# Second FFN's gate and up: chunks begun with one to three weight tiles, seven block products for one weight tile of seven pairs, x kept in DRAM meanwhile

## Chip, cores and metric

One core of a Trainium2 chip. The metric is the device time of one execution in microseconds (us); less is better. TensorE (PE) multiplies, its weight loads (PEld) overlap its matmuls; VectorE (DVE), ScalarE (ACT) and GpSimd (POOL) do the rest; SyncE (SP) issues the DMAs, in the order of its queue.

## The reference

One block of a transformer on 256 tokens of width D = 2048, all in float32. `c` gives nine vectors (shift, scale, gate for each of three parts) by one product with `w_ada`, 144 rows of 128 values.

```python
ada = silu(c) @ w_ada + b_ada
sh1, sc1, g1, shm, scm, gm, sh2, sc2, g2 = split(ada, 9)
h = rms_norm(x, ffn1_norm) * (1 + sc1) + sh1
x = x + 0.5 * g1 * swiglu(h, ffn1_w_gu, ffn1_w_down)
h = rms_norm(x, mix_norm) * (1 + scm) + shm
x = x + gm * hybrid_mixer(h, ...)        # attention and a causal convolution
h = rms_norm(x, ffn2_norm) * (1 + sc2) + sh2
x = x + 0.5 * g2 * swiglu(h, ffn2_w_gu, ffn2_w_down)

def swiglu(h, w_gu, w_down):             # w_gu 2048 x 11264, w_down 5632 x 2048
    g, u = split(h @ w_gu, 2)
    return (silu(g) * u) @ w_down
```

## The kernel before, in words

Stages: first FFN, mixer, second FFN (`ffn(norm2, ...)`, its modulation rows 96 to 127, its gate's 128 to 143). The change is in the last.

Precision: every operand is split in a high and a low part (`whi`, `wlo` of a weight, `hh`, `hl` of an activation), and a product of a 128x128 block of the activation with a 128x512 block of the weight is three matmuls, high x high, high x low and low x high (`mm3`, L329, L333, L334). ScalarE casts the high half (L305), VectorE subtracts for the low (L307), each for 128x1024, half of a weight tile.

Gate and up: the 11264 columns are 22 chunks of 512 (256 of the gate, 256 of up). A chunk's 2048 rows are four weight tiles `w_gu[c, pc]`, each 1 MB: 128 partitions x 4 x 512, `k` = 4 rows' blocks. A weight tile makes 4 x 2 x 3 = 24 matmuls (`mm_tile`: 4 blocks, 2 halves `t` of the tokens). The first weight tile of a chunk needs only a quarter of the normed activation (`hh[0]`, `hl[0]`), and each further one a quarter more, which needs 8 further rows of the modulation (`ada`, L193: a 1 MB DMA, a multiply and a sum on VectorE; `pieces` and `complete` build the quarter).

In the second FFN all 22 chunks first take their first weight tile (L773), with the sums put away as `parts[c]` (L666); chunks 3, 4 and 5 then take their second (`early`, L798), added by `add_part` (L786). Then `groups` finishes chunk by chunk (L860): remaining weight tiles, then `finish`: sum with the part (L830), silu (L831), product (L832), and, since `CROSSBAR` is on for this FFN, a transposition by DMA: `planes` splits the 16-bit halves (L836), the DMA transposes (L842), ScalarE joins them (L845), `split_from_psum` splits them (L350, L351) into `aT[c]`. `after_tiles(n, fn)` puts `fn` off until n weight tiles have been multiplied. `ada_a` and `ada_b` are the rows of the modulation issued per weight tile in the two parts (0.78, 0.5).

Down product (`down_strassen`): in two passes of 1024 columns over 22 chunks; 7 of them (`SEVEN`) use Winograd's form of Strassen's product, seven block products for eight (21 matmuls for 24), with sums of the activation (`sums_of`), of which `KEPT` are kept for the second pass, and differences of the weights on VectorE (L547 to L550). It adds into x and stores the output.

Buffers: `blk` (28 of 4 KB a partition: parts, normed activation, `aT` and others), `raw` (4, the weight tiles and modulation rows as loaded), `whi` and `wlo` (4 halves each), `tmp` (6), `acc` and `tp` (6 and 2 PSUM banks). x has its own 16 KB (`xall`). The order on each engine is made by a list scheduler from the program order; engines then run their own lists in that order and wait for each other by semaphores.

## Time and profile before

| | |
|---|---|
| median of 3 runs | 1829.34 us (1828.84 to 1831.11) |
| the profiled execution | 1831.11 us, span 1829.3 us |
| granted TensorE clock | 0.999 |
| PE, PEld busy | 1802.8 us (99%), 1484.0 us (81%) |
| DVE, ACT, POOL busy | 1519.9 us (83%), 1008.3 us (55%), 28.3 us (2%) |
| DMA | 501.68 MB, mean 274 GB/s |

The span runs from the first instruction to the last; times in rows are us from its start, means of one instruction in ns. A row of a list of stretches has, for each engine, busy us and in brackets the instructions, then the granted clock, the busy share of the 16 DMA engines and GB/s. A row of a group has the line, the engine, the operation, what it writes and reads, the shape, the count, busy us, mean ns, and idle us before it with what ended it. A row of waits has the waiting engine, tile and line, what it waited for, us in total, times, longest. A row of the timeline has start, duration, engine, line, operation and idle us before it; consecutive instructions of an engine may overlap.

### The profile page before, as it was taken

The page shows a single profiled execution, that of the slowest core. Times are in us where ns is not written, and L with a number is a line of the kernel's source. Part 1 is how long each engine was busy: PE and PEld are TensorE (multiplying, and loading weights), DVE is VectorE, ACT ScalarE, POOL GpSimd, SP SyncE. Part 2 cuts the span into 40 slices and gives each one's busy share as a digit, 9 for nine tenths or more (in the row PEclk, how much of TensorE's full clock was granted, in tenths as well). Part 3 has the DMA queues.
Part 4 walks back from the last instruction along what each step waited for, and adds up shares of the span by engine and source line. Part 5 has one row for each costly group of instructions (what it writes and reads, how often), then busy time and mean ns, then how long its engine had stood idle before and what let it go on. Part 6 is the DMA issues. An engine that isn't in the chain of part 4 may idle for free.

```text
span 1829.3 us, 21896 instructions
## 1 busy us (share of the span) xinstructions
PE 1802.8 (99%) x8117; PEld 1484.0 (81%) x8117; DVE 1519.9 (83%) x2018; ACT 1008.3 (55%) x1521; POOL 28.3 (2%) x29
## 2 busy tenths in 40 slices
PE   7999999999999999999999999999999999999998
PEld 5788888888888887788888787888888888878887
DVE  6889869999898787898999778878887765699877
ACT  6553444444444344566798655664665565555453
POOL 0000000000000000000110100000000000000000
PEclk9999999999999999999999999999999999999999
DMA  9987978888889998775444466889899877655552
GB/s 373 349 307 297 347 274 310 327 314 337 337 330 350 355 343 327 290 261 206 176 147 162 160 254 241 328 337 346 262 313 298 302 242 222 203 207 210 204 214 109
DMA packets 95962, 501.68 MB, mean 274 GB/s; under 512 B 31424, under 2 KB 31856, under 8 KB 38384
## 3 DMA queue, kind: packets, MB, share of 16 engines
q1 hardware_dynamic: 95856, 500.30, 74.4%
q8 instruction: 63, 1.03, 0.2%
q14 instruction: 43, 0.35, 0.1%
HBM read 492.37 MB, written 2.12 MB: 270 GB/s over the span
## 4 chain that ended last, share of the span: by engine, by line
PE 85%; DVE 6%; DMA 4%; ACT 3%; issue 2%; POOL 0%; POOLq 0%; DVEq 0%; SPq 0%; ACTq 0%
PE acc L333 27%; PE acc L334 27%; PE acc L329 27%; DVE wlo L307 2%; DMA tmp<-tmp 1%; DMA xall<-in_x_dram 1%; PE tp L333 1%; PE tp L334 1%; DMA raw<-in_w_ada_dram 1%; PE tp L329 1%; ACT whi L305 1%; PE acc L1137 1%; DVE raw L193 1%; DVE wlo L513 1%; DVE blk L1029 1%
## 5 line engine op out<-in xcount | busy, mean ns | idle before, releaser
L333 PE MATMUL acc<-wlo,blk 128*128 128x512 f32 x2340 | 913.7, 390 | 6.9 <-DVE wlo L307 6.9
L329 PE MATMUL acc<-whi,blk 128*128 128x512 f32 x2343 | 911.4, 392 | 1.9 <-ACT blk L403 1.4
L334 PE MATMUL acc<-whi,blk 128*128 128x512 f32 x2340 | 912.3, 390 | 0.1
L305 ACT CAST whi<-raw 128x1024 fp32r<-128x1024 f32 (+1 forms) x581 | 597.3, 1044 | 473.3 <-PE acc L334 333.9
L307 DVE TENSOR_TENSOR wlo<-raw,whi 128x1024 fp32r<-128x1024 f32 (+1 forms) x581 | 691.1, 1210 | 177.7 <-ACT whi L305 176.6
L333 PEld LDWEIGHTS acc<-wlo,blk 128*128 128x128 f32 x2340 | 439.6, 188 | 103.1 <-DVE wlo L307 12.9
L329 PEld LDWEIGHTS acc<-whi,blk 128*128 128x128 f32 x2343 | 439.9, 188 | 93.4 <-ACT blk L403 1.8
L334 PEld LDWEIGHTS acc<-whi,blk 128*128 128x128 f32 x2340 | 439.3, 188 | 91.9 <-DVE blk L405 0.7
L193 DVE CUSTOM_DVE_ANT_0 raw<-raw,c_bc 128x2048 f32<-128x2048 f32 x142 | 324.2, 2285 | 10.3 <-DMA raw<-in_w_ada_dram 10.3
L512 ACT CAST whi<-raw 128x1024 fp32r<-128x1024 f32 (+1 forms) x56 | 53.0, 947 | 68.4 <-PE tp L334 31.9
L513 DVE TENSOR_TENSOR wlo<-raw,whi 128x1024 fp32r<-128x1024 f32 (+1 forms) x56 | 60.8, 1087 | 19.1 <-ACT whi L512 18.9
L666 ACT COPY blk<-acc 128x512 f32<-128x512 f32 x72 | 42.0, 590 | 62.9 <-PE acc L334 60.2
L1029 DVE SCALAR_TENSOR_TENSOR blk<-blk,cst,blk 128x245 f32<-128x245 f32 (+21 forms) x176 | 70.4, 457 | 0.6 <-ACT blk L1027 0.5
L845 ACT COPY tmp<-tmp 128x1024 uint16<-128x1024 uint16 x22 | 29.8, 1355 | 51.2 <-DMA tmp<-tmp 51.2
L830 DVE TENSOR_TENSOR blk<-acc,blk 128x512 f32<-128x512 f32 x88 | 56.6, 682 | 0.0
L831 ACT ACTIVATE blk<-blk 128x256 f32<-128x256 f32 x88 | 33.7, 413 | 20.5 <-DVE blk L830 20.4
L329 PE MATMUL acc<-blk,blk 128*128 128x512 f32 x104 | 41.3, 401 | 1.2 <-ACT blk L321 1.2
L333 PE MATMUL acc<-blk,blk 128*128 128x512 f32 x100 | 39.1, 391 | 0.6 <-DVE blk L307 0.6
L334 PE MATMUL acc<-blk,blk 128*128 128x512 f32 x100 | 39.0, 392 | 0.0
L351 DVE TENSOR_TENSOR blk<-tmp,blk 128x512 fp32r<-128x512 f32 x22 | 15.1, 688 | 26.0 <-ACT blk L350 26.0
L832 DVE TENSOR_TENSOR blk<-blk 128x256 f32<-128x256 f32 x88 | 33.8, 417 | 0.4 <-ACT blk L831 0.4
L836 ACT COPY tmp<-blk 128x1024 uint16<-128x1024 uint16 x22 | 22.9, 1042 | 14.2 <-DVE blk L832 14.1
(227 smaller groups left out, 1058.7 us busy)
## 6 DMA issues: line engine op xcount, KB each, us to landing
raw<-in_w_gu_dram SPq DMA_DIRECT2D x161, 1024.0 KB, 6.0
raw<-in_w_ada_dram SPq DMA_DIRECT2D x142, 1024.0 KB, 6.3
raw<-in_w_dn_dram SPq DMA_DIRECT2D x88, 1024.0 KB, 5.4
raw<-in_w_in_dram SPq DMA_DIRECT2D x40, 1024.0 KB, 4.8
raw<-in_w_out_dram SPq DMA_DIRECT2D x16, 1024.0 KB, 4.8
raw<-in_w_gu_dram SPq DMA_DIRECT2D x8, 768.0 KB, 6.5
blk<-in_w_gu_dram SPq DMA_DIRECT2D x10, 512.0 KB, 13.5
blk<-gate_line SPq DMA_DIRECT2D x6, 512.0 KB, 4.8
```

Source lines behind the costliest of these rows:

```text
L193: nc.vector.tensor_tensor_reduce(out=raw, in0=raw, in1=c_bc, scale=1.0, scalar=0.0, op0=ALU.mult, op1=ALU.add, accum_out=ada_cols[g][:, j ...
L305: nc.scalar.copy(out=hi[:, :m, :], in_=rw)
L307: nc.vector.tensor_sub(out=lo[:, :m, :], in0=rw, in1=hi[:, :m, :].bitcast(F32))
L329: nc.tensor.matmul(acc, ah, wh, start=start, stop=False)
L333: nc.tensor.matmul(acc, ah, wl, start=False, stop=False)
L334: return nc.tensor.matmul(acc, al, wh, start=False, stop=stop)
L512: nc.scalar.copy(out=hi[:, :n, :], in_=src)
L513: nc.vector.tensor_sub(out=lo[:, :n, :], in0=src, in1=hi[:, :n, :].bitcast(F32))
L666: last_part[0] = nc.scalar.copy(out=parts[c][:, t, :], in_=accs[t])
L830: nc.vector.tensor_add(out=p[:, t, :], in0=accs[t], in1=p[:, t, :])
L832: nc.vector.tensor_mul(out=p[:, t, 256:], in0=p[:, t, :256], in1=p[:, t, 256:])
L1029: nc.vector.scalar_tensor_tensor(out=y[:, d:], in0=u, scalar=w, in1=y[:, d:], op0=ALU.mult, op1=ALU.add)
```

## The change

The second FFN's gate and up take another order. 18 chunks begin with one, two or three weight tiles (`AHEAD_2`) whose sum is put away once; chunks 18 to 21 have no part. The rest goes in the order of `REST_2`. For seven pairs of neighbouring chunks (`PAIRS_2`) the last weight tile (pc = 3) of both is taken first, by `pair_first`: Winograd's seven block products over halves of the tokens, of the rows and of the two chunks; sums of the activation come once from `pair_sums`. Four differences of the weights, seven splits and four partial sums (`kept`, read from a bank that is then added to further) go with it. Odd pairs use two `tp` banks.

`finish` writes the transposition's operands into the chunk's own part, and joins two weight tiles after the DMA (`joined`). x lies in four `blk` buffers (the pool has 32 for 28 and `xall` is gone), loaded in halves; they are written to DRAM during chunks 6 to 9 (`spill`) and fetched back at chunk 16 of each pass of the down product (`fetch`). The modulation's rows come at 0.75 and 0.35 a weight tile, three more during the output projection; from row 32 their bias is added for 8 rows at once, and scales are made for four blocks at once. `KEPT` is 7 for 6. Every other use of `x[n][:, t, :]` becomes `xs(n, t)`; `mm3` and `mm_tile` pass on a flag (`more`) that has no instruction of its own.

```diff
 SEVEN = (3, 5, 8, 10, 13, 15, 17)
-KEPT = 6
+KEPT = 7
 CROSSBAR = {0: False, 96: True}
+AHEAD_2 = (1,) * 10 + (2,) * 4 + (3,) * 4
+REST_2 = (10, 14, 0, 11, 18, 15, 2, 12, 4, 16, 20, 6, 13, 8, 17)
+PAIRS_2 = (0, 2, 4, 6, 8, 18, 20)
...
-    blkp = ctx.enter_context(tc.tile_pool(name="blkp", bufs=28))
+    blkp = ctx.enter_context(tc.tile_pool(name="blkp", bufs=32))
...
-    xall = const.tile([P, NT, D], F32, name="xall")
-    x = [xall[:, :, n * 512:(n + 1) * 512] for n in range(4)]
+    xb = [[blk([P, 1024]) for _ in range(2)] for _ in range(NT)]
+
+    def xs(n, t):
+        return xb[t][n // 2][:, n % 2 * 512:n % 2 * 512 + 512]
+
     first_cols = _COLS["nm"][0]
     nc.sync.dma_start(out=cst[:, :first_cols], in_=small[:, :first_cols])
 
     def load_x(t):
-        return nc.sync.dma_start(out=xall[:, t, :], in_=x_in[t * P:(t + 1) * P, :])
+        for h in range(2):
+            ld = nc.sync.dma_start(out=xb[t][h], in_=x_in[t * P:(t + 1) * P, h * 1024:(h + 1) * 1024])
+        return ld
...
-        if j % 2 == 1:
-            p0, o = _COLS["bada"][0] + j - 1, j % 8 - 1
-            nc.vector.tensor_add(out=ada_cols[g][:, o:o + 2], in0=ada_cols[g][:, o:o + 2], in1=cst[:, p0:p0 + 2])
+        n = 2 if j < 32 else 8
+        if j % n == n - 1:
+            p0, o = _COLS["bada"][0] + j + 1 - n, (j + 1 - n) % 8
...
-        if (base, k) not in mods:
+        if (base, k) not in mods and base > 0:
+            ada_until(base + 2 * k // 8 * 8 + 8)
+            a = ada_cols[(base + 2 * k) // 8]
+            k0 = k // 4 * 4
+            G = scales[:, base // 3 + k0:base // 3 + k0 + 4]
+            nc.vector.scalar_tensor_tensor(out=G, in0=a[:, 0:8:2], scalar=1.0, in1=col(norm)[:, k0:k0 + 4],
+                                           op0=ALU.add, op1=ALU.mult)
+            for i in range(4):
+                mods[base, k0 + i] = (G[:, i:i + 1], a[:, 2 * i + 1:2 * i + 2])
+        elif (base, k) not in mods:
...
                 share()
                 first, last = c == 0, c == NCH - 1
+                if c == 16:
+                    fetch(np_)
...
+    def pair_sums(hh, hl):
+
+        res = []
+        for j in range(2):
+            keep = blk([P, 2, 4, P], F32R)
+            full = tmp([P, 2, S])
+            nc.vector.tensor_add(out=full, in0=hh[:, j:4:2].bitcast(F32), in1=hl[:, j:4:2].bitcast(F32))
+            a11, a21, a12, a22 = full[:, 0, :P], full[:, 0, P:], full[:, 1, :P], full[:, 1, P:]
+            q = tmp([P, 4, P])
+            nc.vector.tensor_add(out=q[:, 0], in0=a21, in1=a22)
+            nc.vector.tensor_sub(out=q[:, 1], in0=q[:, 0], in1=a11)
+            nc.vector.tensor_sub(out=q[:, 2], in0=a11, in1=a21)
+            nc.vector.tensor_sub(out=q[:, 3], in0=a12, in1=q[:, 1])
+            hi, lo = keep[:, 0], keep[:, 1]
+            nc.scalar.copy(out=hi, in_=q)
+            nc.vector.tensor_sub(out=lo, in0=q, in1=hi.bitcast(F32))
+            res.append([(hi[:, i], lo[:, i]) for i in range(4)])
+        return res
+
+    def pair_first(w_gu, c, pc, act, sums, banks, parts):
+
+        raws = []
+        for n in range(2):
+            raw = rawp.tile([P, 4, 512], F32, tag="raw", name=nm("raw"))
+            w_dma[0] = nc.sync.dma_start(out=raw, in_=w_gu[c + n, pc].rearrange("p (k n) -> p k n", k=4))
+            raws += [raw[:, 0:2, :], raw[:, 2:4, :]]
+        b11, b21, b12, b22 = raws
+        c11, c21, c12, c22 = banks
+
+        def split(src):
+            hi = whp.tile([P, 2, 512], F32R, tag="whi", name=nm("whi"))
+            lo = wlp.tile([P, 2, 512], F32R, tag="wlo", name=nm("wlo"))
+            nc.scalar.copy(out=hi, in_=src)
+            nc.vector.tensor_sub(out=lo, in0=src, in1=hi.bitcast(F32))
+            return hi, lo
+
+        def times(acc, a, w, start=False):
+            for j in range(2):
+                mm3(acc, a(j), (w[0][:, j, :], w[1][:, j, :]), start and j == 0, j == 1, more=not start)
+
+        def kept(acc, n, t):
+            if parts[c] is None:
+                u = tmp([P, 512])
+                nc.scalar.copy(out=u, in_=acc)
+                return u
+            u = parts[c + n][:, t, :]
+            nc.vector.tensor_add(out=u, in0=acc, in1=u)
+            return u
+
+        k0 = 4 * pc
+        t2 = blk([P, 2, 512])
+        nc.vector.tensor_sub(out=b12, in0=b12, in1=b11)
+        nc.vector.tensor_sub(out=t2, in0=b22, in1=b12)
+        times(c22, lambda j: act(k0 + j, 0), split(b11), True)
+        u11 = kept(c22, 0, 0)
+        nc.vector.tensor_sub(out=b11, in0=t2, in1=b11)
+        times(c12, lambda j: sums[j][0], split(b12), True)
+        u22 = kept(c12, 1, 1)
+        times(c22, lambda j: sums[j][1], split(t2))
+        u12 = kept(c22, 1, 0)
+        nc.vector.tensor_sub(out=t2, in0=b21, in1=t2)
+        times(c21, lambda j: act(k0 + 2 + j, 1), split(t2), True)
+        times(c11, lambda j: act(k0 + 2 + j, 0), split(b21), True)
+        times(c22, lambda j: sums[j][2], split(b11))
+        u21 = kept(c22, 0, 1)
+        times(c12, lambda j: sums[j][3], split(b22))
+        tick()
+        tick()
+        return u11, u21, u12, u22
+
+    xd = dramp.tile([P, NT, 2, 1024], F32, name="x_kept")
+
+    def spill(i):
+        if i < 2 * NT:
+            nc.sync.dma_start(out=xd[:, i // 2, i % 2], in_=xb[i // 2][i % 2])
+
+    def fetch(h):
+        for t in range(NT):
+            xb[t][h] = blk([P, 1024])
+            nc.sync.dma_start(out=xb[t][h], in_=xd[:, t, h])
+
     def ffn(st, w_gu, w_dn, gate_base, ada_a, ada_b, nxt, again, early, early_3):
...
-            for c in range(3, NCH):
-                w = w_tile(w_gu[c, 0])
-                stage_a(c, w, [acc_tile() for _ in range(NT)], (0, 1))
-                ada_a_share(4)
-                pieces()
+            for c, n in enumerate(AHEAD_2):
+                start_of[c] = n
+                if c < 3:
+                    continue
+                accs = [acc_tile() for _ in range(NT)]
+                for pc in range(n):
+                    ada_until(base + 8 * pc + 8)
+                    pieces(last_part[0] if ada_next[0] >= base + 32 else None)
+                    w = w_tile(w_gu[c, pc])
+                    mm_tile(accs, w, act, 4 * pc, pc == 0, pc == n - 1)
+                    ada_a_share(4)
+                    pieces(last_part[0] if ada_next[0] >= base + 32 else None)
+                parts[c] = blk([P, NT, 512])
+                for t in range(NT):
+                    last_part[0] = nc.scalar.copy(out=parts[c][:, t, :], in_=accs[t])
+                spill(c - 6 if c >= 6 else 9)
 
         def segments(c, first, last):
...
-            return left + [(pc, (0, 4)) for pc in range(max(first, 1), last)]
+            return left + [(pc, (0, 4)) for pc in range(max(first, 1) if base == 0 else first, last)]
...
-        def finish(c, accs):
-            p = parts[c]
+        def finish(c, accs, us=None):
+            p = parts[c] or blk([P, NT, 512])
+            m = tmp([P, NT, 256]) if CROSSBAR[base] else p[:, :, 256:]
             for t in range(NT):
-                nc.vector.tensor_add(out=p[:, t, :], in0=accs[t], in1=p[:, t, :])
-                nc.scalar.activation(out=p[:, t, :256], in_=p[:, t, :256], func=AF.Silu)
-                nc.vector.tensor_mul(out=p[:, t, 256:], in0=p[:, t, :256], in1=p[:, t, 256:])
-
+                gu = p[:, t, :] if us or parts[c] else accs[t]
+                if us or parts[c]:
+                    nc.vector.tensor_add(out=gu, in0=accs[t], in1=us[t] if us else gu)
+                nc.scalar.activation(out=p[:, t, :256], in_=gu[:, :256], func=AF.Silu)
+                nc.vector.tensor_mul(out=m[:, t, :], in0=p[:, t, :256], in1=gu[:, 256:])
             if CROSSBAR[base]:
-                planes = tmp([P, 2, NT, 256], U16)
-                nc.scalar.copy(out=planes, in_=p[:, :, 256:].bitcast(U16).rearrange("p t (f b) -> p b t f", b=2))
+                planes, turned = p[:, 0, :].bitcast(U16), p[:, 1, :].bitcast(U16)
+                nc.scalar.copy(out=planes.rearrange("p (b f) -> p b f", b=2),
+                               in_=m.rearrange("p t f -> p (t f)").bitcast(U16).rearrange("p (f b) -> p b f", b=2))
 
             def rest():
+                if CROSSBAR[base]:
+                    nc.sync.dma_start_transpose(out=turned.rearrange("p (j s) -> p j s", s=P), in_=planes)
+                    after_tiles(2, joined)
+                    return
+                tp = tp_tile((P, 2, S))
+                for t in range(NT):
+                    for i in range(2):
+                        nc.tensor.transpose(tp[:, i, t * P:(t + 1) * P], m[:, t, i * P:(i + 1) * P], ident)
+                halves(tp)
+
+            def joined():
+                src = p[:, 0, :].rearrange("p (i t s) -> p i t s", i=2, t=NT)
+                nc.scalar.copy(out=src.bitcast(U16).rearrange("p i t (s b) -> p b t i s", b=2),
+                               in_=turned.rearrange("p (b t i s) -> p b t i s", b=2, t=NT, i=2))
+                halves(src.rearrange("p i t s -> p i (t s)"))
+
+            def halves(src):
                 a = blk([P, 2, 2, S], F32R)
-                if CROSSBAR[base]:
-                    turned = tmp([P, 2, NT, 2, P], U16)
-                    nc.sync.dma_start_transpose(out=turned.rearrange("p b t i s -> p (b t i) s"),
-                                                in_=planes.rearrange("p b t f -> p (b t f)"))
-                    src = tmp([P, 2, NT, P])
-                    nc.scalar.copy(out=src.bitcast(U16).rearrange("p i t (s b) -> p b t i s", b=2), in_=turned)
-                    src = src.rearrange("p i t s -> p i (t s)")
-                else:
-                    src = tp_tile((P, 2, S))
-                    for t in range(NT):
-                        for i in range(2):
-                            nc.tensor.transpose(src[:, i, t * P:(t + 1) * P],
-                                                p[:, t, 256 + i * P:256 + (i + 1) * P], ident)
                 split_from_psum(src, a[:, 0], a[:, 1])
                 aT[c] = a
 
             after_tiles(1, rest)
 
-        groups = [[0, 1, 2]] + [[c] for c in range(3, NCH)]
+        groups = [[0, 1, 2]] + [[c] for c in range(3, NCH)] if base == 0 else [[c] for c in REST_2]
         pend = []
-        for g in groups:
+        pairs = 0
+        for i_g, g in enumerate(groups):
+            if base > 0 and i_g == 1:
+                ada_until(base + 32)
+                pieces(last_part[0])
+                for t in range(NT):
+                    st.complete(3, t)
+                sums = pair_sums(st.hh[3], st.hl[3])
+            if base > 0 and g[0] in PAIRS_2:
+                c = g[0]
+                banks = [acc_tile(), acc_tile()]
+                banks += [tp_tile(), tp_tile()] if pairs % 2 else [acc_tile(), acc_tile()]
+                pairs += 1
+                us = pair_first(w_gu, c, 3, act, sums, banks, parts)
+                ada_share(2 * ada_b[0], ada_b[1])
+                while pend:
+                    finish(*pend.pop(0))
+                for pc in range(start_of[c], 3):
+                    for n in range(2):
+                        w = w_tile(w_gu[c + n, pc])
+                        mm_tile(banks[2 * n:2 * n + 2], w, act, 4 * pc, False, pc == 2, more=True)
+                        ada_share(ada_b[0], ada_b[1])
+                for n in range(2):
+                    pend.append((c + n, banks[2 * n:2 * n + 2], us[2 * n:2 * n + 2]))
+                continue
             accs = {c: [acc_tile() for _ in range(NT)] for c in g}
...
+        if pc == 3:
+            ada_share(1.0, 108)
...
-    ffn(norm2, w_gu2, w_dn2, 128, (0.78, 128), (0.5, 144), None, [], [[3], [4], [5]], [])
+    ffn(norm2, w_gu2, w_dn2, 128, (0.75, 128), (0.35, 144), None, [], [], [])
```

More of the change, by code (lines that the diff above doesn't have):

```diff
@@ L324, in w_first, with mm3 @@
         return [lambda j, i=i: (hi[:, i, :], lo[:, i, :]) for i in range(n)], split
-    def mm3(acc, a, w, start, stop, lo_last=False):
+    def mm3(acc, a, w, start, stop, lo_last=False, more=False):
         ah, al = a
         wh, wl = w
-        nc.tensor.matmul(acc, ah, wh, start=start, stop=False)
+        nc.tensor.matmul(acc, ah, wh, start=start, stop=False, skip_group_check=more)
         if lo_last:
@@ L332, in mm3 @@
             return nc.tensor.matmul(acc, ah, wl, start=False, stop=stop)
-        nc.tensor.matmul(acc, ah, wl, start=False, stop=False)
-        return nc.tensor.matmul(acc, al, wh, start=False, stop=stop)
+        nc.tensor.matmul(acc, ah, wl, start=False, stop=False, skip_group_check=more)
+        return nc.tensor.matmul(acc, al, wh, start=False, stop=stop, skip_group_check=more)
     last_mm = [None]
@@ L420, in begin_norm @@
             self.xn = tmp([P, 512])
-            nc.scalar.activation(out=self.xn, in_=x[0][:, t, :], func=AF.Identity, scale=self.r[t])
+            nc.scalar.activation(out=self.xn, in_=xs(0, t), func=AF.Identity, scale=self.r[t])
         def begin_transposes(self, t):
```

44 lines of the change are left out of this document (23 added, 21 removed).

## Prediction

> **What bounds the kernel now.** I read the page's head first, then TensorE's start times, then busy time by stage, then the groups of the second FFN, then the waits.
>
> ```profile
> span 1829.3 us, 21896 instructions
> PE 1802.8 (99%) x8117; PEld 1484.0 (81%) x8117; DVE 1519.9 (83%) x2018; ACT 1008.3 (55%) x1521; POOL 28.3 (2%) x29
> ...
> 1094.79 0.39 PE L333 MATMUL acc<-blk,blk 128*128 128x512 f32 x1
> ...
> 1100.46 0.39 PE L334 MATMUL acc<-blk,blk 128*128 128x512 f32 x1
> ```
>
> TensorE is busy 99% of the span, but a busy TensorE is not one at its peak. The two matmul rows are the first and the last of 26 in an unbroken run: 5.67 us over 25 steps, so a 128x512 matmul costs 0.2268 us of the path (its own 0.39 us overlaps the next). The loss shows in the weight loads.
>
> ```profile
> core 0: us, PE busy (x) PEld busy (x) DVE busy (x) ACT busy (x) POOL busy (x), PEclk, DMA share, GB/s
> 1050.00:1100.00 50.00, 49.69 (x218) 40.59 (x217) 34.95 (x38) 28.20 (x39) 0.00 (x0) 1.00 0.65 245
> 1120.00:1275.00 155.00, 155.00 (x695) 128.01 (x694) 129.06 (x148) 86.36 (x115) 0.00 (x0) 1.00 0.91 346
> 1275.00:1450.00 175.00, 173.85 (x765) 142.74 (x764) 139.79 (x165) 107.37 (x129) 0.00 (x0) 1.00 0.89 294
> 1450.00:1595.00 145.00, 145.00 (x641) 120.09 (x640) 91.85 (x108) 85.48 (x99) 0.00 (x0) 1.00 0.68 227
> 1480.00:1490.00 10.00, 10.00 (x46) 8.29 (x45) 4.92 (x6) 6.57 (x8) 0.00 (x0) 1.00 0.88 306
> 1597.00:1712.00 115.00, 114.41 (x503) 93.64 (x502) 101.37 (x137) 63.26 (x70) 0.00 (x0) 1.00 0.57 212
> 1712.00:1810.00 98.00, 98.00 (x434) 81.18 (x433) 83.27 (x88) 50.83 (x54) 0.00 (x0) 1.00 0.51 191
> ...
> 1640.00:1650.00 10.00, 10.00 (x46) 8.29 (x45) 10.00 (x15) 6.22 (x7) 0.00 (x0) 1.00 0.49 202
> ```
>
> At full pace weight loads are busy 8.29 of 10 us, 0.829 per us (1480 to 1490). By that measure the second FFN's gate and up (1120 to 1595) lose (128.5 - 128.01)/0.829 = 0.6 us in the first stretch, (145.1 - 142.74)/0.829 = 2.8 us in the second, 0.1 us in the third: 3.5 us in all. So this stage is TensorE at its pace; only fewer matmuls can shorten it much, and VectorE has to keep up. That it can is seen from 1640 to 1650: VectorE 10.00 of 10 us busy, TensorE at full pace.
>
> **The change, part by part.**
>
> *Fewer matmuls.* A weight tile of two chunks took 2 x 4 x 2 x 3 = 48 matmuls; `pair_first` takes 7 products x 2 x 3 = 42. Seven pairs save 42 matmuls: 42 x 0.2268 = **-9.5 us**, on the path. The Trainium skill (TensorE: Matmul & The Clock Gate, "Back-to-back issue gap") puts a 128x512 matmul at about 216 ns alone and about 131 ns in a stream of loads and matmuls; by these the term would be -9.1 or -5.5 us. The trace's 0.2268 us is near the first and contradicts the second, and it decides.
>
> *What VectorE pays for it.* Its instructions overlap too, so I take starts, and the groups for the other kinds:
>
> ```profile
> 1070.35 1.23 DVE L307 TENSOR_TENSOR blk<-raw,blk 128x1024 fp32r<-128x1024 f32 x1 [0.47 <-ACT blk L305]
> 1071.49 1.22 DVE L307 TENSOR_TENSOR wlo<-raw,whi 128x1024 fp32r<-128x1024 f32 x1
> ...
> 1073.76 0.68 DVE L1348 TENSOR_TENSOR tmp<-acc,blk 128x512 f32<-128x512 f32 x1
> 1074.36 1.21 DVE L307 TENSOR_TENSOR wlo<-raw,whi 128x1024 fp32r<-128x1024 f32 x1
> ...
> 1119.12 2.29 DVE L193 CUSTOM_DVE_ANT_0 raw<-raw,c_bc 128x2048 f32<-128x2048 f32 x1
> 1121.33 2.29 DVE L193 CUSTOM_DVE_ANT_0 raw<-raw,c_bc 128x2048 f32<-128x2048 f32 x1
> ...
> L830 DVE TENSOR_TENSOR blk<-acc,blk 128x512 f32<-128x512 f32 x44 | 28.3, 682 | 0.0
> L832 DVE TENSOR_TENSOR blk<-blk 128x256 f32<-128x256 f32 x44 | 17.0, 418 | 0.4 <-ACT blk L831 0.4
> L351 DVE TENSOR_TENSOR blk<-tmp,blk 128x512 fp32r<-128x512 f32 x21 | 14.5, 688 | 26.0 <-ACT blk L350 26.0
> L488 DVE TENSOR_TENSOR tmp<-tmp 128x128 f32<-128x128 f32 x8 | 2.3, 284 | 0.1
> ```
>
> Start to start: 1.14 us for 128x1024, 0.60 for 128x512, 2.21 for one row of the modulation; each is 0.08 under its duration, so 0.34 for 128x256, 0.20 for 128x128, 0.61 for the cast's rest.
> A pair's first tile: 7 low halves and 4 subtractions, 11 x 1.14 = 12.5, and 4 partial sums x 0.60 = 2.4 (on ScalarE for pairs 18 and 20, which have no part yet): 14.9 us, with its 0.7 modulation rows 16.5, against 9.5 us of TensorE: **7.0 us behind**. Each plain tile regains 5.44 - 2 x 1.14 - 0.35 x 2.21 = 2.4 us; each finished chunk costs 2 x (0.60 + 0.34) + 0.61 = 2.5.
> The whole second part (44 plain tiles, 7 pairs, 22 chunks, 16 modulation rows, and `pair_sums` at 2 x (0.60 + 4 x 0.20 + 0.61) = 4.0): 100 + 100 + 55 + 35 + 4 = 294 us of VectorE beside (44 x 24 + 7 x 42) x 0.2268 = 306 us of TensorE, 96%. By full durations instead of starts it is 320 us, 104%. So VectorE is close to being the bound there, but not over it by the rows of starts.
>
> What a burst costs when the average fits is shown by the down product, which has such chunks already: per chunk 6.4 us of VectorE in the second pass (0.60 + 4 x 1.14 + 2 x 0.60), 8.4 in the first with its sums (+2.0), against 21 x 0.2268 = 4.8. The first pass (burst 3.6, seven times; 1597 to 1712) lost (95.3 - 93.64)/0.829 = 2.0 us, the second (burst 1.6; 1712 to 1810) 0.1. A line through both, 0.13 us lost per us of burst, gives 0.73 us for a burst of 7.0: seven pairs, **+5.1 us**. Bounds: 0.1 (second pass) and +13.5 (320 - 306). I take 5.1, as the same mechanism, extrapolated; `split` buffers hold the same four halves in both.
>
> *Old stalls that go.*
>
> ```profile
> 1320.00:1330.00 10.00, 9.64 (x43) 7.63 (x42) 9.07 (x11) 6.35 (x8) 0.00 (x0) 1.00 0.91 323
> 1420.00:1430.00 10.00, 9.40 (x41) 7.80 (x42) 6.83 (x8) 7.32 (x8) 0.00 (x0) 1.00 0.93 336
> ...
> ACT tmp L845 <- DMA tmp<-tmp: 49.5, 21, 4.3
> ...
> tmp<-tmp SPq DMA_TRANSPOSE x21, 4.6
> ...
> 1305.41 8.84 DMA tmp<-tmp
> ...
> 1408.41 7.89 DMA raw<-in_w_ada_dram
> ```
>
> ScalarE stands 49.5 us before L845 (21 times, up to 4.3), waiting for the transposing DMA, with the weight casts behind it in its queue. TensorE's 2.8 us lie largely in the two stretches shown (weight loads 7.63 and 7.80 for 8.29), soon after a transposing DMA took 8.84 us for a median of 4.6 and a modulation row 7.89. `joined` now comes two tiles later, and modulation falls from 0.5 to 0.35 rows per tile, in a stretch where DMAs are 0.89 busy: **-2.5 us** (0 to -3.5). Late next would be the pairs' splits, counted above.
>
> *First part.* 30 weight tiles instead of 22 + 3 come before the rest, the rows of the modulation at 0.75 a tile for 0.78; 18 parts are written out instead of 22, and no `add_part`: both off the path, ScalarE and VectorE are busy 86 and 129 of 155 us there. The spill adds 2 MB to about 53 MB: hidden by what 0.91 leaves; unhidden, 2 MB at 346 GB/s is 6 us.
>
> *Three modulation rows moved into the output projection.* 3 x 2.21 = 6.6 us of VectorE, where it is busy 35 of 50 us, and three 1 MB DMAs on SP's queue, where the next FFN's first tiles stand behind them; DMA is 0.65 busy. 0; if the entry waits for one row, +2.2.
>
> *x in DRAM, fetched back in the down product.* 2 MB in 4 DMAs on SP's queue, weights behind them. DMAs are 0.57 and 0.51 busy: 0. If a fetch had to wait for a free buffer, 1 MB at 212 GB/s is 4.9 us a pass.
>
> *x loaded in halves; KEPT 7; bias and scale in groups of 8 and 4.*
>
> ```profile
> 1.18 0.42 SPq L128 DMA_DIRECT2D xall<-in_x_dram  x1
> ...
> 14.15 0.22 DVE L252 SCALAR_TENSOR_TENSOR ada<-adah,cst 128x1 f32<-128x1 f32 x1
> 14.47 0.46 ACT L403 ACTIVATE blk<-tp,ada,scales 128x128 fp32r<-128x128 f32 x1 [0.28 <-DVE ada L252]
> ...
> 19.20 0.69 DVE L357 CUSTOM_DVE_ANT_0 tmp<-xall 128x512 f32<-128x512 f32 x1 [0.21 <-DMA xall<-in_x_dram]
> ```
>
> The first product waits for the modulation at 14.15, not for x, so x in halves gives 0; at best a pair of squares runs earlier (-1.3), at worst two more issues push the rest (+0.8). KEPT 7 saves one 2.0 us set of sums where TensorE is at full pace, 0 (down to -1.6 if it reaches the end). The grouped additions take some 60 tiny VectorE instructions out, off the path: 0.
>
> **Sum.** -9.5 + 5.1 - 2.5 = -6.9 us. The profiled execution took 1831.11 us (span 1829.3, 1.8 around it), 1.8 above the median of 1829.34, so 1824.2 for it and **1822 us** on the median's scale. 0.2%, 3.7 us, is about what can be told from no change.
>
> **Rivals.**
> 1. *No price for the bursts*: VectorE enters each pair fully ahead, as in the second pass of the down product. -9.5 - 3.5 + 0.1: 1816 us. For: the averages fit (96%). Against: a burst of 7.0 us is four times that pass's.
> 2. *VectorE becomes the bound of the second part*: 320 us by full durations, +13.5 - 9.5 - 2.5: 1831, no change. For: the first pass at 10.00 of 10 us. Against: that same window had TensorE at full pace.
> 3. *The partial sums block the queue* (slower). In `pair_first` four sums wait for a product's end; the next low halves stand behind them on VectorE.
>
> ```profile
> DVE blk L786 <- PE acc L334: 4.3, 5, 1.4
> ```
>
> `add_part` (L786), which has the same form, waited five times, up to 1.4 us. If the sums are issued ahead of the next splits, VectorE and TensorE take turns and the pair runs at VectorE's 14.9 us: +5.4 in each of seven, +38 - 9.5 - 2.5: 1855 us. It decides from 12/7 = 1.7 us a pair (no gain), 2.2 a pair (slower by 0.2%). Against: the splits need no product and may be put ahead. The Trainium skill (same page, the table that opens it) says that VectorE and ScalarE issue strictly in order while TensorE may pull weight loads ahead; the waits of 1.4 us agree.
> 4. *The change does not shorten the path* because another stage's schedule moves (the entry +2.2, a fetch +4.9): 1822 + 7 = 1829.
>
> **How the numbers follow.** Forecast and its near misses (1818 to 1825.6): 0.45; rival 1: 0.17; rivals 2 and 4 (1825.7 to 1833): 0.21; rival 3, from 1833 up: 0.17. Faster 0.62, same 0.21, slower 0.17. Range 1814 to 1834: 0.03 lie below, 0.15 above; cases of both signs are in it, the likeliest one's own is 1818 to 1825.6.
>
> **What would show it.** After: about 8075 matmuls; from the first pair on VectorE over 90% busy, weight loads 1 to 3% under 0.829 per us there; the waits for the turned tile on ScalarE near 0; 42 matmuls of a pair in 10 to 11 us. Wrong if a pair takes over 11.2 us (rival 2 or 3), if VectorE waits for the end of products inside pairs (3), or if TensorE stands at the second FFN's entry or at the fetches (4).

## The result, and the profile after

The changed kernel takes 1847.6 us (median; 1846.0 to 1850.0), the kernel before on the same chip 1829.1: ratio 1.0101, 95% interval 1.0083 to 1.0118. It is 18 us slower, outside the range of 1814 to 1834. The profiled execution took 1847.07 us. That of the kernel before, 1831.11 us, was the slowest of its four, so a difference of 1 or 2 us between single traces says little.

The head of the page of the changed kernel:

```profile
span 1845.3 us, 21902 instructions
PE 1800.0 (98%) x8075; PEld 1477.3 (80%) x8075; DVE 1577.7 (86%) x2021; ACT 1030.8 (56%) x1543; POOL 27.4 (1%) x29
```

The 42 matmuls are gone (8117 to 8075), yet the span is 16 us longer. The time is lost in the second FFN's gate and up. This is the view by windows from the first pair on, 1280 to 1600 us, first of the kernel before, then of the changed one. A column gives busy us and, in brackets, instructions.

```profile
core 0: us, PE busy (x) PEld busy (x) DVE busy (x) ACT busy (x) POOL busy (x), PEclk, DMA share, GB/s
1280.00:1600.00 320.00, 318.85 (x1404) 262.84 (x1403) 229.59 (x268) 192.99 (x225) 0.00 (x0) 1.00 0.80 264
```

```profile
1280.00:1600.00 320.00, 301.84 (x1285) 242.43 (x1283) 278.59 (x311) 203.84 (x236) 0.00 (x0) 0.98 0.72 246
```

In the same 320 us TensorE makes 1285 matmuls instead of 1404. Full pace is 1414 (the first experiment shows it), so 129 are missing: 129 x 0.2268 = 29 us, or 4.2 us in each of seven pairs, where a pair saves 6 x 0.2268 = 1.36 us. VectorE is 49 us busier and still idles for 41 us of the 320. The pairs differ: by the starts of the matmuls they lost 4.7, 1.6, 8.2, 2.2, 3.3, 6.5 and 2.2 us. The second and the fifth, with 1.6 and 3.3, are those whose partial sums ScalarE takes.

What TensorE and ScalarE wait for in the changed kernel from 1240 to 1625 us (total, times, longest):

```profile
PE acc L347 <- ACT whi L692: 6.9, 9, 2.2
PE acc L347 <- ACT whi L323: 5.1, 2, 4.5
PE acc L351 <- DVE wlo L325: 4.8, 3, 3.0
PE acc L347 <- DVE blk L706: 1.1, 1, 1.1
...
ACT blk L966 <- DMA blk<-blk: 15.1, 11, 3.2
```

L692 and L693 make the high and low parts of a pair's weights and L706 its partial sums; L323 and L325 make the parts of a plain tile. So TensorE waited 8.0 us for what the pairs make and 9.9 us for the operands of the tiles just behind them. ScalarE's waits for the turned tile (L966) fell from 51.2 us in the same stretch of the kernel before to 15.1 us. The later joining alone did not do that: in the first experiment below, which has it but no pairs, they are 43.0 us.

```profile
ACT blk L966 <- DMA blk<-blk: 43.0, 21, 4.4
```

The third pair, the costliest, shows how the loss comes about. VectorE's timeline of the changed kernel (start, duration, engine, line):

```profile
1381.06 1.22 DVE L711 TENSOR_TENSOR raw<-raw,raw 128x1024 f32<-128x1024 f32 x1
...
1382.53 1.22 DVE L712 TENSOR_TENSOR blk<-raw 128x1024 f32<-128x1024 f32 x1
1383.72 1.23 DVE L693 TENSOR_TENSOR wlo<-raw,whi 128x1024 fp32r<-128x1024 f32 x1
1384.86 1.22 DVE L715 TENSOR_TENSOR raw<-blk,raw 128x1024 f32<-128x1024 f32 x1
...
1387.73 1.22 DVE L720 TENSOR_TENSOR blk<-raw,blk 128x1024 f32<-128x1024 f32 x1
...
1391.35 3.49 DVE L693 TENSOR_TENSOR wlo<-raw,whi 128x1024 fp32r<-128x1024 f32 x3
1394.76 2.28 DVE L201 CUSTOM_DVE_ANT_0 raw<-raw,c_bc 128x2048 f32<-128x2048 f32 x1
```

From 1381 to 1400 us VectorE hardly pauses. Four subtractions (L711, L712, L715, L720) stand among the low parts, the last three low parts come out only from 1391 us on, and a modulation row and the finishing of the chunk before follow. ScalarE, which casts the high parts, is nearly full as well (9.72 us from 1385 to 1395, in the windows below), but it depends on VectorE: over the seven pairs its casts waited 6.7 us for the last subtraction (L720). SP's queue meanwhile:

```profile
1380.61 0.57 SPq L312 DMA_DIRECT2D raw<-in_w_gu_dram  x1
1384.65 1.24 SPq L955 DMA_TRANSPOSE blk<-blk  x1
1393.73 1.85 SPq L312 DMA_DIRECT2D raw<-in_w_gu_dram  x2
```

No weight load is issued for 13 us. At first, until 1384.65, a transposition that waits for ScalarE stands ahead in the queue. Then the load (L312) waits 7.7 us for the pair's low parts, which give the weight buffers back. The sum of this wait from 1280 to 1600 us, in the changed kernel and then without the four subtractions (an experiment below):

```profile
SPq L312 <- DVE wlo L693: 51.2, 10, 12.4
```

```profile
SPq L312 <- DVE wlo L693: 42.3, 9, 12.0
```

Such a pause alone is not the loss: without the subtractions it is 9.7 us long at this pair, and the whole stage loses only 6 us. Here the next tile lands when TensorE has nothing left. ScalarE's cast of it, and TensorE's matmuls before and after:

```profile
1400.60 1.04 ACT L323 CAST whi<-raw 128x1024 fp32r<-128x1024 f32 x1 [1.82 <-DMA raw<-in_w_gu_dram]
```

```profile
1396.60 0.61 PE L347 MATMUL acc<-whi,blk 128*128 128x512 f32 x2
1401.70 0.78 PE L347 MATMUL acc<-whi,blk 128*128 128x512 f32 x2 [4.48 <-ACT whi L323]
1402.27 0.63 PE L351 MATMUL acc<-wlo,blk 128*128 128x512 f32 x1
1402.70 0.63 PE L352 MATMUL acc<-whi,blk 128*128 128x512 f32 x1
```

TensorE stands for 4.48 us, and from 1402.27 us on a matmul starts every 0.43 us instead of every 0.227. The 5-us windows over this pair:

```profile
1385.00:1390.00 5.00, 4.57 (x20) 3.29 (x18) 4.94 (x6) 4.74 (x6) 0.00 (x0) 1.00 0.28 54
1390.00:1395.00 5.00, 4.42 (x17) 3.30 (x18) 5.00 (x6) 4.98 (x7) 0.00 (x0) 1.00 0.09 16
1395.00:1400.00 5.00, 2.22 (x10) 1.50 (x8) 5.00 (x8) 0.90 (x2) 0.00 (x0) 1.00 0.93 305
1400.00:1405.00 5.00, 3.30 (x9) 2.62 (x10) 3.40 (x6) 3.25 (x4) 0.00 (x0) 0.72 0.76 311
```

Read down the columns: VectorE full, the DMAs (the last but one column) falling to 0.09, TensorE falling to 10 matmuls (24 at full pace), and then the granted clock at 0.72. About 5 of the 29 us are such clock loss, summed over 5-us windows.

### The profile page after: what moved, and what is told of

The parts are those of the page before. It is cut to its first block, busy times and chain, and to the rows that moved or that the text cites. A ratio compares the mean times of both kernels' runs of the same rounds, so it can differ in the third digit from the quotient of the medians.

```text
span 1845.3 us, 21902 instructions
## 1 busy us (share of the span) xinstructions
PE 1800.0 (98%) x8075; PEld 1477.3 (80%) x8075; DVE 1577.7 (86%) x2021; ACT 1030.8 (56%) x1543; POOL 27.4 (1%) x29
## 5 line engine op out<-in xcount | busy, mean ns | idle before, releaser
L347 PE MATMUL acc<-whi,blk 128*128 128x512 f32 x2249 | 876.9, 393 | 17.9 <-ACT whi L692 6.9
L351 PE MATMUL acc<-wlo,blk 128*128 128x512 f32 x2246 | 879.7, 392 | 10.7 <-DVE wlo L325 10.5
L352 PE MATMUL acc<-whi,blk 128*128 128x512 f32 x2246 | 877.7, 391 | 0.1
L323 ACT CAST whi<-raw 128x1024 fp32r<-128x1024 f32 x553 | 571.3, 1046 | 517.5 <-PE acc L352 351.5
L325 DVE TENSOR_TENSOR wlo<-raw,whi 128x1024 fp32r<-128x1024 f32 x553 | 657.3, 1210 | 156.0 <-ACT whi L323 154.5
L347 PEld LDWEIGHTS acc<-whi,blk 128*128 128x128 f32 x2249 | 422.9, 188 | 110.2 <-ACT whi L692 10.7
L351 PEld LDWEIGHTS acc<-wlo,blk 128*128 128x128 f32 x2246 | 423.3, 188 | 104.7 <-DVE wlo L325 15.8
L352 PEld LDWEIGHTS acc<-whi,blk 128*128 128x128 f32 x2246 | 422.9, 188 | 88.5 <-DVE blk L424 0.7
L531 ACT CAST whi<-raw 128x1024 fp32r<-128x1024 f32 (+1 forms) x56 | 53.0, 947 | 66.1 <-PE tp L352 31.9
L532 DVE TENSOR_TENSOR wlo<-raw,whi 128x1024 fp32r<-128x1024 f32 (+1 forms) x56 | 60.9, 1088 | 19.1 <-ACT whi L531 18.8
L1172 DVE SCALAR_TENSOR_TENSOR blk<-blk,cst,blk 128x247 f32<-128x247 f32 (+21 forms) x176 | 70.5, 459 | 0.0
L351 PE MATMUL tp<-wlo,blk 128*128 128x512 f32 x163 | 63.5, 390 | 0.0
L352 PE MATMUL tp<-whi,blk 128*128 128x512 f32 x163 | 63.4, 389 | 0.0
L347 PE MATMUL tp<-whi,blk 128*128 128x512 f32 x163 | 63.2, 389 | 0.0
L945 DVE TENSOR_TENSOR blk<-acc,blk 128x512 f32<-128x512 f32 x76 | 49.3, 683 | 1.9 <-PE acc L352 1.8
L693 DVE TENSOR_TENSOR wlo<-raw,whi 128x1024 fp32r<-128x1024 f32 x35 | 41.5, 1219 | 5.1 <-ACT whi L692 5.1
L692 ACT CAST whi<-raw 128x1024 fp32r<-128x1024 f32 x35 | 35.4, 1050 | 13.1 <-PE acc L352 8.8
```

The lines of the kernel that those rows point to most:

```text
L323: nc.scalar.copy(out=hi[:, :m, :], in_=rw)
L325: nc.vector.tensor_sub(out=lo[:, :m, :], in0=rw, in1=hi[:, :m, :].bitcast(F32))
L347: nc.tensor.matmul(acc, ah, wh, start=start, stop=False, skip_group_check=more)
L351: nc.tensor.matmul(acc, ah, wl, start=False, stop=False, skip_group_check=more)
L352: return nc.tensor.matmul(acc, al, wh, start=False, stop=stop, skip_group_check=more)
L531: nc.scalar.copy(out=hi[:, :n, :], in_=src)
```

## Experiments

The theory after the first look: the burst of VectorE's work in each pair is what costs. By burst I mean VectorE's work at a pair beyond what fits beside the pair's matmuls, some 7 us by the prediction. The rivals: the two weight tiles that a pair holds, where a plain tile is one; the rest of the change (order of chunks, x, the start); the partial sums in VectorE's queue (rival 3 of the prediction). This last falls by the trace: VectorE waited for products in L706 2.1 us in all.

```profile
DVE blk L706 <- PE acc L352: 1.8, 1, 1.8
...
DVE blk L706 <- PE tp L352: 0.3, 1, 0.3
```

In what follows "missing" is 1414 less the matmuls of the window 1280 to 1600, times 0.2268 us. Stage lengths, which some expectations use, give about the same per pair. The kernels ran in several sessions, so each is held against the kernel before of its own session, by the ratio.

**No pairs.** Everything else of the change stays.

```diff
-PAIRS_2 = (0, 2, 4, 6, 8, 18, 20)
+PAIRS_2 = ()          # the 14 chunks put back as plain ones into REST_2
-                sums = pair_sums(st.hh[3], st.hl[3])
```

> The changed kernel without its pairs: all 22 chunks one by one in the same order, everything else of the change kept (2112 matmuls). Theory A (the pairs alone cost the time, 27 us of lost TensorE pace in the second part): 1825 to 1829 us. Rival B (the new order, the writing and fetching of x, the three modulation rows or the deferred joining cost it): 1838 us or more.

Measured: 1830.41 us, ratio 1.0018 (1.0009 to 1.0027).

```profile
1280.00:1600.00 320.00, 320.00 (x1414) 264.96 (x1413) 223.32 (x253) 196.01 (x227) 0.00 (x0) 1.00 0.81 260
```

TensorE never stands. So in this stage the rest of the change works: the 10 matmuls (2.3 us) that the kernel before was missing are there. The time lies just over its expectation of 1825 to 1829 us. The pairs cost 0.8%, 15 us, of the 18; the rest of the change costs about 3.

**One pair alone** (chunks 4 and 5).

```diff
+PAIRS_2 = (4,)
```

> The changed kernel with one pair only, chunks 4 and 5, the other chunks one by one. Theory A1 (each pair's burst of VectorE work stalls TensorE by itself, about 4 us a pair, also where VectorE has a full lead before it): no pairs - 1.4 + 4, so 2 to 3 us over the run without pairs. Rival A2 (only the average load counts: seven pairs bring VectorE to 96% and more, and its lead never comes back): the single pair is hidden, 1 to 1.5 us under the run without pairs.

Measured: 1830.42 us, ratio 1.0019 (1.0009 to 1.0028), 1409 matmuls in the window: 1.1 us missing. A pair with plain chunks all round it loses about what it saves (1.36 us), so the total does not change. Both expectations miss: it does not lose the 4 us of the first, nor is it free as in the second. The same pair loses 2.2 us among seven, so how full VectorE is around a pair counts as well.

**Without the four subtractions.** This leaves out a part of the computation: the products take the tiles as loaded. The loads, the splits, the partial sums and the 42 matmuls stay.

```diff
-        nc.vector.tensor_sub(out=b12, in0=b12, in1=b11)
-        nc.vector.tensor_sub(out=t2, in0=b22, in1=b12)
...
-        nc.vector.tensor_sub(out=b11, in0=t2, in1=b11)
...
-        nc.vector.tensor_sub(out=t2, in0=b21, in1=t2)
```

> All seven pairs, the four subtractions of the weights left out (the products take the weights as loaded, so part of the computation is left out): VectorE's burst falls by 4 x 1.14 = 4.6 us a pair, the number of products, splits and partial sums stays. Theory A1 (VectorE's burst): most of 27 us comes back, 1824 to 1830 us. Rival C (the two weight buffers that a pair holds to its end keep the next weights from loading, whatever VectorE does): more than half of the loss stays, 1836 us or more.

Measured: 1824.35 us, ratio 0.9984 (0.9974 to 0.9993): 1.2%, 21 us, under the changed kernel, with only VectorE's work and the waits for its results taken away.

```profile
1280.00:1600.00 320.00, 317.26 (x1387) 258.66 (x1386) 268.46 (x313) 221.11 (x260) 0.00 (x0) 1.00 0.77 264
```

27 matmuls missing, 6.1 us, 0.9 a pair, under the 1.36 that a pair saves. The subtractions decide; the pairs' banks, loads and order cost little by themselves.

**Half the burst.** The last two of the four left out (again a part of the computation).

```diff
-        nc.vector.tensor_sub(out=b11, in0=t2, in1=b11)
...
-        nc.vector.tensor_sub(out=t2, in0=b21, in1=t2)
```

> The changed kernel with two of the four subtractions of each pair left out (b11 = t2 - b11 and t2 = b21 - t2; the products then take b11 and b21 as they were loaded, so a part of the computation is changed). The burst of a pair falls from 4 to 2 subtractions more than plain splits. With none of them a pair's stall was 0.9 us, with four 4.2. A line between the two (the price is VectorE time, microsecond by microsecond): 2.5 us a pair, 12 us less than the changed kernel, near 1836 us. A knee (operand buffers absorb the first part of a burst, and past them the clock falls too): 1.2 us a pair or less, 1826 to 1828 us.

Measured: 1828.64 us, ratio 1.0006 (0.9997 to 1.0015).

```profile
1280.00:1600.00 320.00, 313.58 (x1365) 254.24 (x1364) 277.44 (x321) 218.59 (x258) 0.00 (x0) 1.00 0.79 259
...
1390.00:1395.00 5.00, 3.83 (x17) 2.73 (x16) 4.89 (x8) 3.13 (x5) 0.00 (x0) 1.00 0.64 265
1395.00:1400.00 5.00, 5.00 (x24) 4.14 (x23) 5.00 (x5) 3.85 (x4) 0.00 (x0) 1.00 0.97 306
```

49 missing: 11.1 us, 1.6 a pair. With 0, 2 and 4 subtractions a pair loses 0.9, 1.6 and 4.2 us: the first two cost 0.7 us for 2 x 1.14 = 2.3 us of VectorE, the last two 2.6 us, more than their own time. That is between the two expectations and nearer the knee: at the third pair the DMAs keep on (0.64, 0.97) and the clock stays at 1.00, where the whole burst had 0.09 and 0.72. VectorE's busy share does not show it: 277.44 us here and 278.59 in the changed kernel, with 18 us of difference in what TensorE lost. The two left out are also the later ones in the pair, so size and place are not separated by this run.

**Subtractions on GpSimd.**

```diff
-        nc.vector.tensor_sub(out=b12, in0=b12, in1=b11)
+        nc.gpsimd.tensor_sub(out=b12, in0=b12, in1=b11)      # and so the other three
```

> The four subtractions of each pair on GpSimd instead of VectorE, nothing left out. Theory A1: VectorE is relieved by the same 4.6 us a pair, so the time falls towards that of the run without subtractions if GpSimd takes at most about 1.5 us for one; if it takes more than 2.5 us, the products wait for GpSimd and the time stays at 1845 us or more. Rival C (held buffers): 1843 us or more in either case.

Measured: 1871.69 us, ratio 1.0238 (1.0223 to 1.0253), the worst of all. Groups of that kernel, GpSimd's first subtraction and VectorE's low parts, and then the spread of L325 (minimum, median, maximum in ns):

```profile
L711 POOL TENSOR_TENSOR raw<-raw,raw 128x1024 f32<-128x1024 f32 x7 | 19.7, 2814 | 364.5 <-DVE wlo L325 200.7 <-DMA raw<-in_w_gu_dram 163.8
```

```profile
L325 DVE TENSOR_TENSOR wlo<-raw,whi x104: 1208/1222/3424, 1242.5 to 1638.0; 128x1024 fp32r<-128x1024 f32 x104
```

A subtraction takes 2.81 us there, and ScalarE's casts waited 10.1 us for the last one (L720). TensorE waited longest for VectorE's partial sums (L706), 17.9 us. The move does not even free VectorE: from 1280 to 1600 us it is busy for 278.39 us, in the changed kernel for 278.59, beside 1192 matmuls instead of 1285. Single low parts grew from 1.22 to 3.42 us, by 2.2 us. The Trainium skill ("SBUF — State Buffer", section "SBUF: two separate sides") says that VectorE's operations with two inputs from SBUF and GpSimd's share a pair of ports that one instruction holds to its end while the other blocks; the 2.2 us agree. The sums that read a PSUM bank (L945) met a subtraction 18 times and stayed at 0.68 us.

**One weight tile held instead of two.** The pair's second tile is neither loaded nor used (a part of the computation is changed); the four subtractions stay.

```diff
+        raw = rawp.tile([P, 4, 512], F32, tag="raw", name=nm("raw"))
+        w_dma[0] = nc.sync.dma_start(out=raw, in_=w_gu[c, pc].rearrange("p (k n) -> p k n", k=4))
+        b11, b21 = raw[:, 0:2, :], raw[:, 2:4, :]
+        b22 = b21
+        b12 = blk([P, 2, 512])
```

> All seven pairs with one weight tile for both chunks (the second chunk's last weight tile is left out, its first difference goes to a spare buffer), so that a pair holds one of the four weight buffers instead of two and loads 1 MB less; VectorE and ScalarE do the same 11 x 1.14 + 4 x 0.60 us. Theory A1 (VectorE's burst alone): 1842 us or more. Theory C (the held weight buffers turn the burst into a late load and a second stall): 1836 us or less. Between them, both.

Measured: 1845.05 us, ratio 1.0094 (1.0079 to 1.0109): no change against 1.0101.

```profile
1280.00:1600.00 320.00, 303.33 (x1292) 243.41 (x1291) 279.40 (x313) 205.81 (x238) 0.00 (x0) 0.98 0.67 224
...
1390.00:1395.00 5.00, 3.12 (x9) 1.96 (x10) 5.00 (x7) 3.98 (x5) 0.00 (x0) 0.92 0.00 0
```

At the third pair the DMAs stop all the same, and the stage loses as much. So it is not how many tiles the pair holds.

**Fewer modulation rows in the second part.** Some of them are moved into the output projection; VectorE's 278.59 us in the window fall to 267.05, five rows of 2.28.

```diff
-        if pc == 3:
-            ada_share(1.0, 108)
+        if pc > 0:
+            ada_share(1.0, 113)
...
-    ffn(norm2, w_gu2, w_dn2, 128, (0.75, 128), (0.35, 144), None, [], [], [])
+    ffn(norm2, w_gu2, w_dn2, 128, (0.75, 144), (0.35, 144), None, [], [], [])
```

> The changed kernel with more of the modulation's rows ahead of the pairs: 9 instead of 3 in the output projection, and the limit of 128 in the first part lifted, so that some 9 rows instead of 16 are left beside the pairs (15 us less of VectorE there, and fewer weight buffers taken). Theory A1 (burst): a pair's burst loses at most its own 0.7 row, 1844 to 1847 us. Theory A2 (average load decides): 7 x 2.2 = 15 us less comes back in large part, 1836 to 1840 us.

Measured: 1854.21 us, ratio 1.0149 (1.0133 to 1.0164), worse than either expectation. The window of the output projection, first of the changed kernel, then of this one:

```profile
1050.00:1085.00 35.00, 34.94 (x154) 28.61 (x153) 30.82 (x30) 21.57 (x26) 0.00 (x0) 1.00 0.84 320
```

```profile
1050.00:1085.00 35.00, 27.56 (x113) 21.97 (x112) 26.80 (x26) 16.32 (x22) 2.67 (x1) 0.90 0.81 294
```

The pairs gained 19 matmuls (1304), 4.3 us. The projection lost 41 matmuls in this window, 9 us, and 56, 12.7 us, from 1000 to 1085 us. The rows cost more there than the pairs gained.

**A weight tile between the parts of a pair** (the last plain tile of the chunks before, put ahead of the fourth subtraction), and **the finishing of the chunks before put off** past the pair's splits (with the modulation rows at 0.4 for 0.35 a tile, none at the pair itself), each alone and both together:

```diff
         u12 = kept(c22, 1, 0)
+        between()             # the last tile of the chunks before
         nc.vector.tensor_sub(out=t2, in0=b21, in1=t2)
```

```diff
                 us = pair_first(w_gu, c, 3, act, sums, banks, parts)
-                ada_share(2 * ada_b[0], ada_b[1])
-                while pend:
-                    finish(*pend.pop(0))
                 for pc in range(start_of[c], 3):
...
+                        while pend:
+                            finish(*pend.pop(0))
```

> The last plain weight tile ahead of a pair is multiplied between the pair's third and fourth product, nothing else changed: VectorE's 14.9 us stand beside 42 + 24 matmuls, 15.0 us, instead of beside 9.5. Theory A1 (burst): most of the stalls go, 1826 to 1834 us. Theory C (held buffers): the pair holds its two weight buffers 5.4 us longer, so it gets no better, 1845 us or more.

> All seven pairs; the chunks finished after a pair's first tile (2.5 us of VectorE each) come one plain tile later, and the 0.7 modulation row issued with a pair's first tile goes to the plain tiles (0.4 for 0.35). Theory A1 (what stands in VectorE's queue during the burst sets the stall): 2 to 4 us of burst less, 1836 to 1843 us. Rival (work moved by one tile is still ahead of the next splits): 1845 us or more.

> All seven pairs with the tile between (1837.5 us) and the finishing and the modulation row deferred. Theory A1: 1830 to 1835 us. Rival (average load: VectorE's work is the same 294 us beside 306): 1837 us or more.

Measured: 1837.52 us, ratio 1.0051 (1.0035 to 1.0068); 1838.02, ratio 1.0054 (1.0037 to 1.0070); both together 1833.26, ratio 1.0030 (1.0020 to 1.0040). The first misses its 1826 to 1834, the other two lie where they were expected. The windows in this order:

```profile
1280.00:1600.00 320.00, 309.91 (x1337) 250.25 (x1336) 286.42 (x325) 211.95 (x249) 0.00 (x0) 0.99 0.74 255
```

```profile
1280.00:1600.00 320.00, 311.75 (x1340) 252.19 (x1339) 288.62 (x324) 214.51 (x249) 0.00 (x0) 0.99 0.74 256
```

```profile
1280.00:1600.00 320.00, 314.26 (x1359) 254.93 (x1358) 290.55 (x328) 217.48 (x254) 0.00 (x0) 0.99 0.75 259
```

Here VectorE's total work stays, and only its order changes: 17.5, 16.8 and 12.5 us missing instead of 29. So what costs is when VectorE's work comes, and not only how much it is. Even the best, 1.8 us a pair, is over 1.36. Two more versions of it: the tile between together with the moved rows, and only two pairs, the last two, with the tile between:

> Both of the last two edits. Theory A1: 1 to 4 us under the run with the tile between alone, at best 1823 us. Theory C: fewer modulation rows take weight buffers while a pair holds two, so this one gains more over the tile between than A1 allows, 5 us or more.

> Two pairs only, 18 and 20, whose partial sums ScalarE takes (VectorE 12.5 instead of 14.9 us), with the plain tile between products three and four; the other chunks one by one. Theory A1: about 1 us of stall a pair against 1.4 us saved: 1829 to 1830.5 us, at or just under the run without pairs. If a pair costs what it did with seven (2.3 us with the tile between): 1832 us.

Measured: 1847.32 us, ratio 1.0108 (1.0093 to 1.0123), the projection's loss again, where less than with the tile between alone was expected; and 1831.22, ratio 1.0023 (1.0012 to 1.0034), no better than no pairs.

**x stays in SBUF**, no pairs (28 blocks, no spill and fetch, KEPT 6): of the change the order of the chunks, the later joining and the handling of the modulation's rows are left.

```diff
-    xb = [[blk([P, 1024]) for _ in range(2)] for _ in range(NT)]
+    xall = const.tile([P, NT, D], F32, name="xall")
```

> The run without pairs, with x left in its own buffer as before (28 block buffers, x loaded whole, no writing and fetching, KEPT 6): of the change only the new order, the deferred joining and the modulation's handling stay. Theory D (the 3 us by which the run without pairs is over the kernel before come from x in halves at the start, first product at 16.0 to 17.3 instead of 15.0 us, and from the later stages' buffers): 1825 to 1828 us in this chip's scale, where the run without pairs has 1830.4 and the kernel before 1827.2. Rival (the new order itself costs them): 1829.5 us or more.

Measured: 1828.2 us, ratio 1.0004 (0.9996 to 1.0013), against 1.0018 with x in halves: 2.6 us. It lies just over the first expectation. The first product in the kernel before, in the changed one and in this:

```profile
14.98 0.80 PE L329 MATMUL acc<-whi,blk 128*128 128x512 f32 x1 [1.40 <-ACT blk L403]
```

```profile
8.20 0.69 DVE L376 CUSTOM_DVE_ANT_0 tmp<-blk 128x512 f32<-128x512 f32 x1 [1.51 <-DMA blk<-in_x_dram]
...
16.44 0.80 PE L347 MATMUL acc<-whi,blk 128*128 128x512 f32 x1 [4.46 <-ACT blk L422]
```

```profile
14.64 0.79 PE L345 MATMUL acc<-whi,blk 128*128 128x512 f32 x1 [1.27 <-ACT blk L420]
```

With x in halves the second half is worked on from 8.20 us on, where the whole tile was there at 6.55, and the first product comes 1.5 us later. In the fourteen kernels with halves it comes at 15.74 to 17.60 us, in the three with x whole at 14.64 to 14.98.

With TensorE at full pace for the stage, this kernel still does not beat the kernel before. Part of the reason is the start of the down product, first before, then in this kernel:

```profile
1600.00:1625.00 25.00, 24.41 (x106) 19.09 (x105) 22.76 (x35) 14.77 (x18) 0.00 (x0) 1.00 0.45 169
```

```profile
1600.00:1625.00 25.00, 22.92 (x98) 17.52 (x96) 23.86 (x37) 14.55 (x18) 0.00 (x0) 1.00 0.48 173
```

Eight matmuls, 1.8 of the 2.3 us gained, are lost again. In this kernel's trace SP issues no weight load from 1595.4 to 1605.6 us, behind the gate's line:

```profile
SPq L291 <- ACT tmp L289: 8.6, 1, 8.6
```

**The gate's line on GpSimd's queue**, in this kernel and in the one with both reorderings:

```diff
-            nc.sync.dma_start(out=line, in_=row)
+            nc.gpsimd.dma_start(out=line, in_=row)           # and its two broadcasts
```

> As the kernel without pairs in which x stays in SBUF (1828.2 us), with the gate's line written and broadcast from GpSimd's queue instead of SP's. If the wait for ScalarE's copy of the gate, standing in SP's queue ahead of the next weight tile, is what stops the weight loads for 9 us at the down product's start, that gap goes, TensorE's stops of about 2 us there go, and the time is 1825.5 to 1826.5. If the gap has another cause (full buffers), no change: 1828.

> As the seven pairs with a tile between the parts of each and the finishing put off (1833.3 us), with the gate's line on GpSimd's queue. By the gate's line: 2 us less, 1831. By another cause of the gap: 1833.

Measured: 1831.31 us, ratio 1.0021 (1.0013 to 1.0030), and 1835.75, ratio 1.0048 (1.0034 to 1.0062): not faster, 3 us slower. At the down product's start the wait has a new name and about the same length:

```profile
SPq L310 <- DVE tmp L505: 9.7, 1, 9.7
```

The weight load now waits itself, for VectorE, and from 1600 to 1655 us the kernels with and without the edit make the same 230 matmuls. The gate's line was only first in a queue that had to wait anyway; the theory falls. The slowdown lies elsewhere: the edit moves the mixer's gate line too, and from 1000 to 1085 us, around the output projection, the first of these kernels makes 368 matmuls where the one without the edit makes 397. Why was not looked into. What would shorten the gap at the down product's start stays open.

No version beat both kernels with the whole computation done. More weight buffers, or x in SBUF beside KEPT 7, were not tried.

## Why the prediction was wrong

- **Fewer matmuls, -9.5 us**: right, 8075.
- **Old stalls, -2.5 us**: right in size. The kernel without pairs has no missing matmul where the kernel before had 10, 2.3 us. The reason given is not borne out: ScalarE still waits 43.0 us there for the turned tile (51.2 before), and TensorE does not stand. Which of the new order, the fewer modulation rows and the later joining did it is not separated. The total does not show the gain: 1.8 us go at the start of the down product, and x in halves costs more.
- **The bursts, +5.1 us (0.73 a pair)**: the step that failed. They cost 29 us, 4.2 a pair. The 0.73 came from 0.13 us lost per us of burst, read off the down product's two passes as averages and drawn on as a line. The first pass's loss, though, lies at the first two of its seven bursts; the five after them, as long, cost nothing. The kernel before:

```profile
1610.00:1625.00 15.00, 14.41 (x62) 10.91 (x61) 14.96 (x23) 9.54 (x11) 0.00 (x0) 1.00 0.37 142
1625.00:1712.00 87.00, 87.00 (x385) 72.07 (x384) 77.25 (x101) 47.44 (x52) 0.00 (x0) 1.00 0.59 221
```

In the second row the weight loads are at full pace (87 x 0.829 = 72.1). VectorE is full in the first and not in the second. So the slope was no price of a burst, and the pairs do not follow it: without subtractions, with 2.4 us of burst left, a pair loses 0.9 us where the line gives 0.1. The first two subtractions (2.3 us) add 0.7 us, 0.3 per us; the last two add 2.6, 1.1 per us, nearly nine times the slope. There TensorE waits for the pair's operands and for the tile behind it, and after some of the stops its clock falls.
- **Its upper bound, +13.5 us**, was wrong too, and for a reason of its own. It came from VectorE's sum (320 us of work against TensorE's 306), as if VectorE, once the bound, were always busy. It was busy for 87% of the window (the row of 278.59), not the over 90% that I wrote: after a burst it has times with nothing to do. ScalarE's casts, which VectorE's low parts follow, then wait for weights, 15.8 us in all against 3.0 without pairs:

```profile
ACT whi L323 <- DMA raw<-in_w_gu_dram: 15.8, 8, 3.6
```

That VectorE itself held those loads back is likely by SP's waits, but no run shows it apart.

- **Rival 2** (VectorE as the bound, no change) came nearest as a mechanism, with a price of +13.5 where 29 was right. **Rival 3** had the sign and, at 1855 us, a time nearer than mine, but its mechanism is refuted by 2.1 us of waiting in L706. **Rival 1** is refuted. **Rival 4**: the entry did not suffer, and the fetches were not seen to cost; the 3 us lost outside the pairs are elsewhere.
- **x in halves, 0 (-1.3 to +0.8)**: missed against the kernel with x whole; the ratios with and without halves differ by 2.6 us (KEPT and the spill are in that too). Against the kernel before, the 1.5 us of the first product are made up in the trace by 50 us: 140 matmuls for 138, and 147 with x whole.
- **What would show it**: weight loads 1 to 3% under full pace; 8.5% under (242.43 against 264.96). A pair's 42 matmuls in 10 to 11 us, wrong over 11.2: 9.5 + 4.2 = 13.7 us on average, with the gap behind it. The turned tile's waits near 0: 15.1 us of 51.2 left, but 43.0 without the pairs, so this sign did not show what it was to show.

How the 29 us divide in cause between operands late inside the pair and weights late behind it is not settled: the waits are 8.0 and 9.9 us, but no run held the loads apart from VectorE's order.

## What to carry over

The price of a burst on a helping engine is not its share of an average: ask for how long the main engine can live on what is prepared, and expect each microsecond past that to cost about one (1.1 here). A slope from another stage is worth something only if the loss lies where the bursts are: look at each before averaging. Compare the loss of one occurrence with the gain of one (here 4.2 against 1.36 us), and try half of its cost first; one occurrence alone (1.1 us) would have flattered the seven. Reordering the burst recovered over half, without taking any work away; moving it to GpSimd, or other rows to the output projection, made it worse.
